# Attention scores as 64-row products, two heads in the two halves of the array, and a rotary step with whole heads in a tile

## The chip, the cores and the metric

The kernel runs on one core of a Trainium2 chip. The metric is the device time of one execution in microseconds (us). Before the change it is 1016.0 us, the median of three runs (1015.67 to 1016.91).

A core has five engines with a queue each, worked off in order: TensorE (PE; its weight loads are shown as PEld), VectorE (DVE), ScalarE (ACT), GpSimd (POOL) and SyncE (SP), which here issues the transfers. Engines wait for each other by semaphores. Matrix products go into eight PSUM banks of 128 x 512 float32; everything else lies in SBUF, 128 partitions wide.

## The reference, cut to what matters

A decoder block on 512 tokens of width 1024, in float32: a SwiGLU part, a token-mixing part, a second SwiGLU part, each behind a modulated RMSNorm. The change is in the token mixing:

```
proj = u @ w_in                      # p (256), q, k, v (768 each), gates (2048)
y_pool = multiscale_pool(p, ...)
q = apply_rope(q.reshape(B, S, 12, 64), cos, sin)      # also k
for gi, (window, dilation) in enumerate(((128, 1), (512, 4), (2048, 16))):
    hs = slice(gi * 4, gi * 4 + 4)                     # four heads of 64 per group
    o, lse = dilated_window_attention(q[:, :, hs], k[:, :, hs], v[:, :, hs], window // dilation, dilation)
y_attn = sum of the groups' outputs, weighted by softmax of their lse
merged = g_pool * (y_pool @ w_pool_branch) + g_attn * (y_attn @ w_attn_branch)
return merged @ w_out

def apply_rope(t, cos, sin):
    t1, t2 = jnp.split(t, 2, axis=-1)
    return jnp.concatenate([t1 * cos - t2 * sin, t2 * cos + t1 * sin], axis=-1)
```

Scores are products over the 64 elements of a head, in float32.

## The kernel before, in words

Dense layers are computed with channels on partitions and tokens on the free axis. To keep float32 accuracy at the speed of the rounded type, each operand is split in a high and a low part, and each product is three: high by high, high by low, low by high (`mm3`, L339 to L343; written out in other loops, L1226 to L1228 and L1276 to L1278). Weights come in 512 KB chunks by SP into three buffers (`fetch`, L226). ACT writes their high part (`split_hi`, L298) and DVE their low part (`split_lo`, L310) into a ring. `look` (L319), called at the start of a tile, fetches and keeps the split three chunks ahead of PE. A tile (`mm_tile`) is 24 products of 128 x 512, one PSUM bank.

`mix` runs the token mixing. All instructions stand in each engine's queue in the order in which this Python code emits them: there is no scheduler behind it. Its stages:

- `head` computes q and k of group 0 in four banks; `rope` (L978) turns them on DVE. A tile holds 32 elements of each of four heads: one tile the first halves, one the second. So a rotation needs two tiles, `pa` and `pb`: four products (L985) and, for each pair of heads, a difference (L991) and a sum (L992), that put both halves of the two heads into 128 rows. `classes` = 4 reorders tokens by residue, for groups 1 and 2.
- v of group 0 (L1226 to L1229).
- Eight tiles with q and k of groups 1 and 2. Between their products PE works on the attention of group 0, as hooks at the step k of the tile (`hooks`, L1236). A unit is a block of 128 queries and a pair of heads (n, hp); there are eight in group 0. A unit's work stands in three tiles: scores at hook 5, transposes of the probabilities at hook 3 of the next tile, products with v at hook 4 of the one after. One unit enters per tile.
- Two tiles for the pooling branch (`pool_diff` on POOL), four wide steps for v of groups 1 and 2 (L1276 to L1282). Beside them the units of groups 1 and 2 (kind 1) run in pairs, hp = 0 and 1.
- Gates, the merge of the groups, and the output.

The scores: the rows of a pair of heads are interleaved by halves, so a product over one head alone needs a copy of q with the other head's rows at zero. `at_prep` (L1014) makes it on DVE (L1022) with a mask of ones and zeros, and `at_scores` (L1026) multiplies over all 128 rows, one product per head (and group): L1039, L1041, L1045. Its result lies in one of two banks (`bS`), by turns. DVE adds the mask and takes maxima (L1057, L1059), ACT takes exponentials (L1062). `at_turn` transposes on PE (L1074) and copies on ACT (L1077, L1080). `at_values` (L1083) multiplies with v on PE (L1097) into a half of the bank `bO`, by hp; in group 0 DVE copies that half out at once (L1099), and in groups 1 and 2 both halves after the second (L1101).

Of the kernel before, what the change touches and what calls it, by code (L numbers as in the profile page):

```python
# [75 lines left out]
    return ins, [np.concatenate(outs[i:i + 2], axis=1) for i in range(0, n, 2)] + outs[n:]  # L76


def qk_cols(base, g, second):
    return np.concatenate([base + (4 * g + h) * 64 + 32 * second + np.arange(32) for h in range(4)])  # L80


def lay_mix(w_in, w_pb, w_ab, w_out):
    ch = []

    def qk(g):
        for base in (256, 1024):
            for s in (0, 1):
                ch.append(_fmajor(w_in, qk_cols(base, g, s)))

    qk(0)
    v = w_in[:, 1792:2560].reshape(KT, P, 768)
    for i in range(2):
        ch.append(v[4 * i:4 * i + 4, :, :256].transpose(1, 0, 2).reshape(P, -1))
    qk(1)
    qk(2)
    for t in range(2):
        ch.append(_fmajor(w_in, np.arange(t * P, (t + 1) * P)))
    for i in range(4):
        ch.append(v[2 * i:2 * i + 2, :, 256:].transpose(1, 0, 2).reshape(P, -1))  # L100
    for m in range(KT + 1):
        if m < KT:
            ch.append(_fmajor(w_in, 2560 + np.arange(m * P, (m + 1) * P)))
            ch.append(_fmajor(w_in, 3584 + np.arange(m * P, (m + 1) * P)))
        if m:
            c = np.arange((m - 1) * P, m * P)
            ch.append(np.concatenate([_fmajor(w_pb, c), _fmajor(w_ab, c)], axis=1))
    for m in range(KT):
        ch.append(_fmajor(w_out, np.arange(m * P, (m + 1) * P)))
    return ch  # L110
# [26 lines left out]
class Kernel:  # L137
# [837 lines left out]
        for b in range(4):  # L975
            self.nc.sync.dma_start(self.cs[32 * b:32 * b + 32], self.scr2)

    def rope(self, pa, pb, dst, classes=1):  # L978

        v = self.nc.vector
        t = [self.rt.tile([P, 528], F32, name=f"rt{i}")[:, :T] for i in range(4)]
        for o, x, y in ((t[0], pa, self.cos), (t[1], pb, self.sin), (t[2], pb, self.cos), (t[3], pa, self.sin)):
            v.tensor_tensor(o, x, y, op=OP.mult)  # L985
        for half in (0, 1):
            rows = slice(64 * half, 64 * half + 64)
            cols = slice(T * half, T * half + T)
            src = [x[rows].rearrange("p (i c) -> p c i", c=classes) for x in t]
            to = [dst[r, cols].rearrange("p (c i) -> p c i", c=classes) for r in (slice(0, 64), slice(64, 128))]  # L990
            v.tensor_tensor(to[0], src[0], src[1], op=OP.subtract)  # L991
            v.tensor_tensor(to[1], src[2], src[3], op=OP.add)  # L992

    def mm_tile(self, hooks=()):

# [15 lines left out]
        kind, n, hp = u  # L1011
        return (1, 2) if kind else (0,), slice(n * P, n * P + P)

    def at_prep(self, u):  # L1014

        kind, n, hp = u
        gs, toks = self.at_tokens(u)
        qz = self.aw.tile([P, T], F32, name="qz")
        for i, g in enumerate(gs):
            q = self.qt[g][:, hp * T:hp * T + T]  # L1020
            for h in range(2):
                self.nc.vector.tensor_scalar(qz[:, (2 * i + h) * P:(2 * i + h + 1) * P], q[:, toks],  # L1022
                                             self.hmask[:, h:h + 1], None, op0=OP.mult)
        self.qz[u] = qz

    def at_scores(self, u):  # L1026
        kind, n, hp = u
        nc = self.nc
        M = nc.tensor.matmul
        self.si ^= 1  # L1030
        S = self.bS[self.si]
        qz = self.qz.pop(u)
        gs, toks = self.at_tokens(u)
        for h in range(2):
            o = h * 256
            if kind == 0:
                k = self.kt[0][:, hp * T:hp * T + T]
                if n == 0:
                    M(S[:, o + P:o + 2 * P], qz[:, h * P:h * P + P], k[:, 0:P], start=True, stop=True)  # L1039
                else:  # L1040
                    M(S[:, o:o + 2 * P], qz[:, h * P:h * P + P], k[:, (n - 1) * P:(n + 1) * P], start=True, stop=True)  # L1041
            else:
                for i, g in enumerate(gs):
                    k = self.kt[g][:, hp * T:hp * T + T]
                    M(S[:, o + i * P:o + i * P + P], qz[:, (2 * i + h) * P:(2 * i + h + 1) * P], k[:, toks],  # L1045
                      start=True, stop=True)
        p = self.aw.tile([P, T], F32, name="prob")
        nb = self.aw.tile([P, 2], F32, name="negmax")
        mask = self.mask[kind]
        c0 = P if (kind == 0 and n == 0) else 0  # L1050
        if kind == 0:
            mx, ls = self.m1[:, 4 * n + 2 * hp:4 * n + 2 * hp + 2], self.l1[:, 4 * n + 2 * hp:4 * n + 2 * hp + 2]
        else:
            mx, ls = self.o23[:, n, 256 + 2 * hp:258 + 2 * hp], self.o23[:, n, 260 + 2 * hp:262 + 2 * hp]
        for h in range(2):
            cs = slice(h * 256 + c0, h * 256 + 256)
            nc.vector.tensor_tensor_reduce(p[:, cs], S[:, cs], mask[:, c0:], 1.0, 3.0 * NEG, op0=OP.add, op1=OP.max,  # L1057
                                           accum_out=mx[:, h:h + 1])
        nc.vector.tensor_scalar(nb, mx, -0.125, None, op0=OP.mult)  # L1059
        for h in range(2):  # L1060
            cs = slice(h * 256 + c0, h * 256 + 256)
            nc.scalar.activation(p[:, cs], p[:, cs], AF.Exp, bias=nb[:, h:h + 1], scale=0.125,  # L1062
                                 accum_out=ls[:, h:h + 1])
        self.prob[u] = p
# [112 lines left out]
    def mix(self):  # L1177
        nc, tc = self.nc, self.tc
        v, M = nc.vector, nc.tensor.matmul
        self.prob, self.probT, self.pd, self.qz = {}, {}, {}, {}  # L1180
        self.si = self.ti = 0
        outer = ExitStack()
        mp = outer.enter_context(tc.tile_pool(name="mx", bufs=1))
        two = lambda pool, n, dt=F32R: [pool.tile([P, T], dt, name=f"{n}{i}") for i in range(2)]
# [1 line left out]
        with tc.tile_pool(name="ma", bufs=1) as ma, tc.tile_pool(name="rt", bufs=1) as self.rt, \  # L1186
# [15 lines left out]

            bk = [self.nb() for _ in range(4)]
            self.head(1, bk, AF.Exp)
            self.rope(bk[0], bk[1], self.qt[0])
            self.rope(bk[2], bk[3], self.kt[0])


            free = [b for b in self.B if b not in bk]
# [6 lines left out]
            for n in range(4):  # L1216
                if n:
                    self.split(self.pos + n - 1)
                    self.fetch()
                if n == 3:  # L1220
                    self.at_prep((0, 0, 0))
                b = self.nb()
                ts = slice(n * P, n * P + P)
                for k in range(KT):
                    hi, lo = w[k]
                    M(b[:, :256], self.UH[k][:, ts], hi, start=k == 0, stop=False)  # L1226
                    M(b[:, :256], self.UH[k][:, ts], lo, start=False, stop=False)
                    M(b[:, :256], self.UL[k][:, ts], hi, start=False, stop=k == KT - 1)  # L1228
                nc.scalar.activation(self.v1[:, n, :], b[:, :256], AF.Copy)  # L1229
# [3 lines left out]

            pipe = [[], []]

            def hooks(new, extra=(), nxt=()):  # L1236
                h = {}
                sc, old = pipe
                for i, u in enumerate(old):
                    h.setdefault(4, []).append(lambda u=u: self.at_values(u))  # L1240
                for i, u in enumerate(sc):
                    h.setdefault(3 + i, []).append(lambda u=u: self.at_turn(u))
                for i, u in enumerate(new):
                    if u not in self.qz:
                        h.setdefault(i, []).insert(0, lambda u=u: self.at_prep(u))
                    h.setdefault(5 + i, []).append(lambda u=u: self.at_scores(u))
                for u in nxt:
                    h.setdefault(6 + len(new) - 1, []).append(lambda u=u: self.at_prep(u))
                for k, f in extra:
                    h.setdefault(k, []).append(f)  # L1250
                pipe[0], pipe[1] = list(new), sc
                return h


            todo = [[(0, n, hp)] for n in range(4) for hp in range(2)]
            for g in (1, 2):
                for dst in (self.qt[g], self.kt[g]):
                    ps = [self.mm_tile(hooks(todo.pop(0), nxt=todo[0] if todo else ())) for s in range(2)]
                    self.rope(ps[0], ps[1], dst, 4)


            g23 = [[(1, c, hp) for hp in range(2)] for c in range(4)]
            b = self.mm_tile(hooks([], nxt=g23[0]))
            self.pool_diff(0, b)
            b = self.mm_tile(hooks(g23[0], nxt=g23[1]))
            self.pool_diff(1, b)
            self.held = self.pos
            w = [x for _ in range(4) for x in self.take()]
# [83 lines left out]
    def build(self):  # L1352
# [21 lines left out]
        self.hpi, self.r4 = tl("hpi", 1), tl("r4", 4)  # L1374
        self.cond = tl("cond", D)
        self.ones = tl("ones", P)
        self.invf, self.hmask, self.icnt, self.ident = cst[:, 0:1], cst[:, 1:3], cst[:, 3:35], cst[:, 35:163]
        self.cst = cst
        self.cs = tl("cs", 2 * T)
        self.cos, self.sin = self.cs[:, :T], self.cs[:, T:]  # L1380
# [142 lines left out]
def constants():  # L1523
    i = np.arange(P)
    invf = (ROPE_THETA ** (-np.arange(0, HEAD_DIM, 2) / HEAD_DIM)).astype(np.float32)
    hm = np.stack([(i % 64 // 32 == h) for h in range(2)], axis=1).astype(np.float32)
    cnt = np.zeros((P, 32), np.float32)
    for t in range(2):
        for half in range(2):
# [2 lines left out]
                np.float32(1) / np.minimum(np.arange(16) + 1, w).astype(np.float32)  # L1532
    neg = lambda ok: np.where(ok, np.float32(0), np.float32(NEG))
    q, k = i[:, None], i[None, :]
    return np.concatenate([invf[i % 32][:, None], hm, cnt, np.eye(P, dtype=np.float32),
                           neg(k >= q), neg(k <= q), neg((k <= q) & ((q - k) % 4 == 0))], axis=1)


# [40 lines left out]
```

## Time and profile before

| | before |
|---|---|
| median of three runs | 1016.0 us |
| the profiled execution, its own time | 1016.32 us |
| its span, first to last instruction | 1014.5 us |
| PE busy | 1003.8 us |
| DVE busy | 764.8 us |
| ACT busy | 442.0 us |
| mean granted PE clock | 0.998 |
| attention of group 0 beside q and k of groups 1 and 2 | 393 to 457 us of the span |
| attention of groups 1 and 2 | 457 to 509 us |

Busy times are sums over the span; PE's are modelled ends of pipelined products, so two may overlap. A view of instructions in order of time gives the start, the duration, engine, line, operation, output and inputs, and in brackets the idle time before it with what ended it. Lines are those of the kernel before, unless "after" is written.

### The profile page before, as it was taken

How to read it: one execution, taken by the hardware profiler on the slowest of the kernel's cores; microseconds unless marked ns; L12 is line 12 of the kernel's file. 1: busy time of each engine (PE TensorE's matmuls, PEld its weight loads, DVE VectorE, ACT ScalarE, POOL GpSimd, SP SyncE). 2: the span in 40 equal slices, each digit the busy share in tenths (PEclk: the TensorE clock that was granted, in tenths of full speed). 3: DMA queues.
4: the chain of work that ended last, by engine and by line, in shares of the span. 5: the costliest groups of instructions: out<-in, count | busy, mean ns of one | idle time of the engine just before them, and what ended most of it. 6: DMA issues, size and time to landing. Idle time of an engine off the chain costs nothing.

```text
span 1014.5 us, 15763 instructions
## 1 busy us (share of the span) xinstructions
PE 1003.8 (99%) x6448; PEld 912.2 (90%) x6448; DVE 764.8 (75%) x1120; ACT 442.0 (44%) x674; POOL 26.1 (3%) x30
## 2 busy tenths in 40 slices
PE   8999999999999999999999999999999999999997
PEld 7888999989899999889988888998899899998997
DVE  7989979789796667878448776577787776676754
ACT  5443644525435443334323333454366254352553
POOL 0000000000000000008000000000000000000001
PEclk9999999999999999999999999999999999999999
DMA  9856456455454323222155773421353234241312
GB/s 336 274 197 214 146 163 221 148 175 168 148 182 136 104 77 104 63 63 84 32 198 188 253 265 107 122 63 62 95 176 122 66 105 146 84 146 43 113 33 83
DMA packets 43114, 139.61 MB, mean 138 GB/s; under 512 B 4897, under 2 KB 8225, under 8 KB 43042
## 3 DMA queue, kind: packets, MB, share of 16 engines
q1 hardware_dynamic: 42354, 137.95, 41.8%
q8 instruction: 50, 0.82, 0.3%
q10 hardware_dynamic: 688, 0.66, 0.2%
q14 instruction: 22, 0.18, 0.1%
HBM read 135.82 MB, written 2.77 MB: 137 GB/s over the span
## 4 chain that ended last, share of the span: by engine, by line
PE 93%; DVE 5%; ACT 1%; issue 1%; DMA 0%; DVEq 0%; ACTq 0%
PE bank L341 16%; PE bank L342 16%; PE bank L343 16%; PE bank L723 10%; PE bank L725 10%; PE bank L724 10%; PE bank L1506 1%; PE bank L1510 1%; PE bank L1508 1%; PE bank L1097 1%; PE bank L1276 1%; DVE wlo L310 1%; PE bank L1277 1%; PE bank L1278 1%; PE bank L1045 1%; PE bank L1074 1%
## 5 line engine op out<-in xcount | busy, mean ns | idle before, releaser
L310 DVE TENSOR_TENSOR wlo<-raw,whi 128x1024 fp32r<-128x1024 f32 (+6 forms) x166 | 174.4, 1062 | 66.5 <-ACT whi L298 65.9
L298 ACT ACTIVATE whi<-raw 128x1024 fp32r<-128x1024 f32 (+6 forms) x166 | 150.0, 920 | 47.6 <-DVE raw L242 41.6
L725 PE MATMUL bank<-UH,wlo 128*128 128x256 f32 x544 | 150.5, 277 | 0.0
L723 PE MATMUL bank<-UH,whi 128*128 128x256 f32 x544 | 150.5, 277 | 0.0
L724 PE MATMUL bank<-UL,whi 128*128 128x256 f32 x544 | 150.5, 277 | 0.0
L341 PE MATMUL bank<-HI,whi 128*128 128x512 f32 (+1 forms) x406 | 146.6, 361 | 0.0
L342 PE MATMUL bank<-HK,whi 128*128 128x512 f32 (+1 forms) x406 | 146.4, 361 | 0.0
L343 PE MATMUL bank<-HI,wlo 128*128 128x512 f32 (+1 forms) x406 | 146.2, 360 | 0.0
L341 PE MATMUL bank<-UH,whi 128*128 128x512 f32 (+1 forms) x400 | 145.9, 365 | 0.0
L343 PE MATMUL bank<-UH,wlo 128*128 128x512 f32 (+1 forms) x400 | 141.8, 355 | 0.5 <-DVE wlo L310 0.5
L342 PE MATMUL bank<-UL,whi 128*128 128x512 f32 (+1 forms) x400 | 141.8, 355 | 0.1
L310 DVE TENSOR_TENSOR wlo<-X,whi 128x1024 fp32r<-128x1024 f32 (+4 forms) x106 | 111.7, 1064 | 33.3 <-ACT whi L298 32.9
L298 ACT ACTIVATE whi<-X 128x1024 fp32r<-128x1024 f32 (+4 forms) x106 | 95.7, 927 | 46.3 <-DVE X L242 45.6
L723 PE MATMUL bank<-SH,whi 128*128 128x256 f32 x408 | 113.8, 279 | 0.1
L724 PE MATMUL bank<-SL,whi 128*128 128x256 f32 x408 | 113.6, 278 | 0.0
L725 PE MATMUL bank<-SH,wlo 128*128 128x256 f32 x408 | 113.6, 278 | 0.0
L724 PEld LDWEIGHTS bank<-UL,whi 128*128 128x128 f32 x544 | 102.3, 188 | 0.3
L723 PEld LDWEIGHTS bank<-UH,whi 128*128 128x128 f32 x544 | 102.1, 188 | 0.3
L725 PEld LDWEIGHTS bank<-UH,wlo 128*128 128x128 f32 x544 | 102.1, 188 | 0.0
L342 PEld LDWEIGHTS bank<-HK,whi 128*128 128x128 f32 x406 | 76.3, 188 | 11.8 <-DVE HK L651 0.4
L341 PEld LDWEIGHTS bank<-HI,whi 128*128 128x128 f32 x406 | 76.5, 188 | 11.5
L343 PEld LDWEIGHTS bank<-HI,wlo 128*128 128x128 f32 x406 | 76.4, 188 | 11.6
(228 smaller groups left out, 1760.2 us busy)
## 6 DMA issues: line engine op xcount, KB each, us to landing
ada<-wada SPq DMA_DIRECT2D x47, 512.0 KB, 5.0
raw<-wmix SPq DMA_DIRECT2D x44, 512.0 KB, 3.6
raw<-wf1i SPq DMA_DIRECT2D x32, 512.0 KB, 4.4
raw<-wf2i SPq DMA_DIRECT2D x30, 512.0 KB, 3.6
X<-wf2i SPq DMA_DIRECT2D x14, 512.0 KB, 3.6
cs<-wada SPq DMA_DIRECT2D x12, 512.0 KB, 3.5
AR<-wada SPq DMA_DIRECT2D x12, 512.0 KB, 4.2
raw<-wf2o SPq DMA_DIRECT2D x12, 512.0 KB, 3.6
```

The source lines that it names most:

```text
L298: self.nc.scalar.activation(self.hi[:, y], r[:, x], AF.Copy)
L310: self.nc.vector.tensor_tensor(self.lo[:, y], r[:, x], self.hi[:, y], op=OP.subtract)
L341: M(ps, hi, uh, start=start, stop=False)
L342: M(ps, hi, ul, start=False, stop=False)
L343: M(ps, lo, uh, start=False, stop=stop)
L723: M(o, hi, uh, start=start and p == 0 and k == 0, stop=False, skip_group_check=True)
L724: M(o, hi, ul, start=False, stop=False, skip_group_check=True)
L725: M(o, lo, uh, start=False, stop=k == 3, skip_group_check=True)
L1045: M(S[:, o + i * P:o + i * P + P], qz[:, (2 * i + h) * P:(2 * i + h + 1) * P], k[:, toks], start=True, stop=True)
L1074: nc.tensor.transpose(b[:, i * P:i * P + P], p[:, i * P:i * P + P], self.ident)
L1097: M(o, pt[:, blk * P:blk * P + P], v, start=i == 0, stop=i == len(srcs) - 1)
L1276: M(b, self.UH[k][:, c::4], hi, start=k == 0, stop=False)
```

## The change

Rows of the projection are laid out by whole heads: a tile now holds two heads of 64, each with its first 32 rows, then its second 32. The rotation works on one tile at a time. ACT copies the bank to SBUF with the sign of the sine term; four transfers on SP's queue exchange the 32-row halves within SBUF; DVE multiplies the bank with the cosines (`rope_a`), and later the exchanged copy with the sines, and adds (`rope_b`). In group 0 all four `rope_a` stand before the four `rope_b`; in groups 1 and 2 each `rope_b` stands right behind its `rope_a`.

The masked copies of q (`at_prep`) are gone. A score product runs over the 64 rows of its head, rows 0 to 63 for the first head and 64 to 127 for the second, each head into a bank of its own, and the two units hp = 0 and 1 of a pair into the halves of these banks. The units of group 0 enter in pairs, one pair every second tile: `todo` holds [pair, nothing, pair, nothing, ...]. Both units' scores stand at hook 5, one behind the other, then both units' maxima and exponentials (`at_exp`). Values are as before in their text: for each unit of the pair at hook 4, products into its half of `bO`, then DVE's copy.

```diff
     def qk(g):
         for base in (256, 1024):
-            for s in (0, 1):
-                ch.append(_fmajor(w_in, qk_cols(base, g, s)))
+            for hp in (0, 1):
+                ch.append(_fmajor(w_in, base + (4 * g + 2 * hp) * 64 + np.arange(P)))
...
-    def rope(self, pa, pb, dst, classes=1):
-        v = self.nc.vector
-        t = [self.rt.tile([P, 528], F32, name=f"rt{i}")[:, :T] for i in range(4)]
-        for o, x, y in ((t[0], pa, self.cos), (t[1], pb, self.sin), (t[2], pb, self.cos), (t[3], pa, self.sin)):
-            v.tensor_tensor(o, x, y, op=OP.mult)
-        for half in (0, 1):
...
+    def rope_a(self, bank, dst, hp, classes, t, w):
+        nc = self.nc
+        nc.scalar.activation(t, bank, AF.Copy, scale=self.sign)
+        for i in range(4):
+            o = i ^ 1
+            nc.sync.dma_start(w[32 * o:32 * o + 32], t[32 * i:32 * i + 32])
+        by = lambda x: x.rearrange("p (i c) -> p c i", c=classes)
+        nc.vector.tensor_tensor(dst[:, hp * T:hp * T + T].rearrange("p (c i) -> p c i", c=classes), by(bank), by(self.cos),
+                                op=OP.mult)
+
+    def rope_b(self, dst, hp, classes, w):
         v = self.nc.vector
+        d = dst[:, hp * T:hp * T + T].rearrange("p (c i) -> p c i", c=classes)
+        v.tensor_tensor(w, w, self.sin, op=OP.mult)
+        v.tensor_tensor(d, d, w.rearrange("p (i c) -> p c i", c=classes), op=OP.add)
...
-    def at_prep(self, u):
...
     def at_scores(self, u):
         kind, n, hp = u
         nc = self.nc
         gs, toks = self.at_tokens(u)
+        for i, g in enumerate(gs):
+            for h in range(2):
+                rows = slice(64 * h, 64 * h + 64)
+                q, k = (x[g][rows, hp * T:hp * T + T] for x in (self.qt, self.kt))
+                if kind:
+                    o, ks = slice(i * P, i * P + P), toks
                 else:
+                    o, ks = (slice(0, 2 * P), slice((n - 1) * P, (n + 1) * P)) if n else (slice(P, 2 * P), toks)
+                S = self.bS[h][:, 2 * P * hp:2 * P * hp + 2 * P]
+                nc.tensor.matmul(S[:, o], q[:, toks], k[:, ks], start=True, stop=True, skip_group_check=True)
...
+            to = [(self.qt[0], 0), (self.qt[0], 1), (self.kt[0], 0), (self.kt[0], 1)]
+            sw = [self.qt[2][:, :T], self.qt[2][:, T:], self.kt[2][:, :T], self.kt[2][:, T:]]
+            for i in range(4):
+                self.rope_a(bk[i], *to[i], 1, self.v23[:, i, :], sw[i])
+            for i in range(4):
+                self.rope_b(*to[i], 1, sw[i])
...
-                for i, u in enumerate(new):
-                    if u not in self.qz:
-                        h.setdefault(i, []).insert(0, lambda u=u: self.at_prep(u))
-                    h.setdefault(5 + i, []).append(lambda u=u: self.at_scores(u))
-                for u in nxt:
-                    h.setdefault(6 + len(new) - 1, []).append(lambda u=u: self.at_prep(u))
+                h.setdefault(5, []).extend(lambda f=f, u=u: f(u) for f in (self.at_scores, self.at_exp) for u in new)
...
-            todo = [[(0, n, hp)] for n in range(4) for hp in range(2)]
+            todo = [x for n in range(4) for x in ([(0, n, hp) for hp in range(2)], [])]
             for g in (1, 2):
                 for dst in (self.qt[g], self.kt[g]):
-                    ps = [self.mm_tile(hooks(todo.pop(0), nxt=todo[0] if todo else ())) for s in range(2)]
-                    self.rope(ps[0], ps[1], dst, 4)
+                    for hp in range(2):
+                        b = self.mm_tile(hooks(todo.pop(0)))
+                        rt = [self.rt.tile([P, 528], F32, name=f"rt{2 * i + hp}")[:, :T] for i in range(2)]
+                        self.rope_a(b, dst, hp, 4, *rt)
+                        self.rope_b(dst, hp, 4, rt[1])
```

`at_exp` is the second part of the old `at_scores`, from the maxima on. The constants hold the signs where the masks of ones and zeros were.

## The prediction, made before the changed kernel had run

> **What bounds the kernel now.** I read the page first, then the waits of TensorE, then the attention part (381 to 515 us) in order of time, engine by engine, then the order of instructions and semaphore waits in both built programs.
>
> ```profile
> span 1014.5 us, 15763 instructions
> PE 1003.8 (99%) x6448; PEld 912.2 (90%) x6448; DVE 764.8 (75%) x1120; ACT 442.0 (44%) x674; POOL 26.1 (3%) x30
> PE 93%; DVE 5%; ACT 1%; issue 1%; DMA 0%; DVEq 0%; ACTq 0%
> ```
>
> TensorE is the bound everywhere: 1003.8 of 1014.5 us busy, 93% of the chain that ended last. So a microsecond taken from its queue is a microsecond gained, and a wait put into its queue is lost in full; the other engines matter only where PE waits for them. In the attention part PE waits only once in a visible way, for an exponential:
>
> ```profile
> 413.98 0.39 PE L343 MATMUL bank<-UH,wlo 128*128 128x512 f32 x1
> 414.61 0.93 PE L1074 MATMUL bank<-cst,prob 128*128 128x128 f32 x4 [0.24 <-ACT prob L1062]
> ```
>
> The start before the gap is 413.98; a 512-column product is followed 0.227 us later, so L1074 could start at 414.21 and started at 414.61; its four pieces then took 0.68 to the next line instead of 0.36. That is 0.7 us, the slack of this schedule at its tightest.
>
> **What the scores cost PE now.** PE in order of time (start, duration):
>
> ```profile
> 409.02 0.40 PE L343 MATMUL bank<-UH,wlo 128*128 128x512 f32 x1
> 409.26 1.02 PE L1041 MATMUL bank<-k,qz 128*128 128x256 f32 x4
> 409.93 0.58 PE L341 MATMUL bank<-UH,whi 128*128 128x512 f32 x1
> 410.36 0.39 PE L342 MATMUL bank<-UL,whi 128*128 128x512 f32 x1
> ...
> 470.82 1.05 PE L1045 MATMUL bank<-k,qz 128*128 128x128 f32 x8
> 471.63 0.60 PE L1276 MATMUL bank<-whi,UH 128*128 128x512 f32 x1
> ```
>
> A float32 product runs as two passes. The 256-column passes stand 0.168 us apart (409.26 to 409.93, four), the 128-column ones 0.10 (470.82 to 471.63, eight); the first wide product after a block is 0.2 us late (409.93 to 410.36 instead of 0.227). A unit costs 0.45 us (n = 0), 0.88 (n > 0) or 1.0 (groups 1 and 2); 2 x 0.45 + 6 x 0.88 + 8 x 1.0 = 14.2 us in all. That is all the change can win from the scores.
>
> **The change, part by part.**
>
> *Scores.* The number of passes stays. The two units of a pair now follow each other in one hook, so half of the late starts go: 3 x 0.2 + 4 x 0.2 + 0.08 = 1.5 us. What two heads in the two halves of the array do is not in the trace. Ceiling: passes in pairs at half the time, 24 x 0.168/2 + 64 x 0.10/2 + 8 x 0.09/2 = 5.6 us. Floor: no gain, and something lost at each of the 16 changes between whole and halved array; the nearest row is the late start of 0.2 us, and with the 0.16 by which a product outlasts its spacing that bounds it at 0.35 each, 5.6 us. I take weight loads as the limit: the closest spacing of any pass here is 0.09 us (transposes L1074, four in 0.36), so 256-column passes fall from 0.168 to 0.09 (24 x 0.078 = 1.9) and 128-column ones by 0.01 (0.6): 2.5 us, less 16 x 0.08 = 1.3 for the changes. Row, then rule: the Trainium skill (TensorEngine Tiling (Array Packing), Key Properties) says that switching the tiling mode drains the TensorE; no trace here shows it. By that rule the late start would be paid on entering as well, 8 x 0.2 = 1.6 in place of 1.3. With the 0.7 us of the exponential's wait (it falls away, below), the scores gain 1.5 + 2.5 - 1.3 + 0.7 = 3.4 us.
>
> *Masked copies (L1022).* 48 DVE operations go, 0.2 to 0.45 us each. PE never waited for them; worth nothing by themselves.
>
> *Rotary step.* Per pair of projection tiles DVE made four products and four half-height operations. Now each tile has one ACT copy (0.60, as L1151), four transfers on SP, and on DVE a product with cosines (strided, 1.08 as L991 in groups 1 and 2), one with sines (0.68 as L985) and an add (1.08). DVE busy falls from 7.0 us per pair (404.31 to 411.5) to 5.7. But DVE now stands still between the first and the second product until the transfers land, and everything behind them in its queue waits: the weight split L310, the copies of the attention output (L1099), the maxima (L1057).
>
> *Group 0.* Four copies end near 382.8, sixteen transfers leave SP from 381.4 at 0.46 us each (to 388.3), land by 390.4; the last two operations end at 391.9, where DVE's L310 began at 391.13 before. PE needs that split near 393.5, and it is there at 393.0: nothing, or 2 us once if transfers land 2 us later.
>
> *Values: the wait that decides.* Units of a pair now turn and multiply in the same tile. Both write halves of one bank (bO), and DVE copies the first half out before the second is written. In the order of the built program PE's first product of the second unit (L1083 after) waits for DVE's copy of the first unit (L1085 after) issued in the same hook. Before, that copy lay a whole tile back (412.69, while PE's next values stood at 416.08). In DVE's queue this copy stands behind the previous tile's rotary step and a weight split:
>
> ```profile
> 410.44 1.07 DVE L992 TENSOR_TENSOR q<-rt,rt 64x512 f32<-64x512 f32 x1
> 411.55 1.23 DVE L310 TENSOR_TENSOR wlo<-raw,whi 128x1024 fp32r<-128x1024 f32 x1
> 412.69 0.28 DVE L1099 COPY o<-bank 128x128 f32<-128x128 f32 x1
> ```
>
> Count from the end of the tile before, 0 = the start of the next tile's first product. ACT starts at 0.2 (a DVE read of a finished bank began 0.20 after, 405.16 to 405.36), ends at 0.8. SP issues four transfers at 0.46 us each (spacing of the four cs<-scr), the fourth at 2.3. Landing:
>
> ```profile
> cs<-scr SPq DMA_DIRECT2D x4, 128.0 KB, 4.2
> out_dram<-out SPq DMA_DIRECT2D x3, 128.0 KB, 1.8
> masks<-cst SPq DMA_DIRECT2D x1, 192.0 KB, 2.4
> ```
>
> No transfer within SBUF is there; bounds 1.8 and 4.2. I take 2.1, between the two rows that did not share the engines: 64 KB rides alone here, since weight loads are issued behind the four. So 4.4, plus 0.1; sine 5.2, add 6.3, split 7.5 (411.55 to 412.69 is 1.14), copy 7.8, PE going again at 8.0 (0.2 as above). PE arrives at 4 x 0.681 + 0.81 = 3.5 (eight passes of values, 423.31 to 424.12; n = 0 has four, 3.1). **Gap: 4.5 us three times, 4.9 once: 18.4 us.** With 1.8 it is 17.2, with 4.2 it is 26.8. While PE stands, DVE catches up, so the exponentials are no longer late.
>
> *The clock in these gaps.* The granted clock after PE's last matmul, which ends at 1007.7 (core: stretch, length, busy times, PEclk, DMA):
>
> ```profile
> 1009.00:1009.50 0.50, 0.00 (x0) 0.00 (x0) 0.50 (x3) 0.00 (x0) 0.50 (x2) 1.00 0.76 260
> 1009.50:1010.00 0.50, 0.00 (x0) 0.00 (x0) 0.50 (x3) 0.00 (x0) 0.50 (x1) 0.90 0.01 2
> 1010.00:1010.50 0.50, 0.00 (x0) 0.00 (x0) 0.38 (x2) 0.00 (x0) 0.09 (x1) 0.50 0.39 135
> ```
>
> It fell to half 2.2 us after the last work. At the start, matmuls ran at the slow duration (421 ns for 128x128, 275 later) from 4.60 to 8.18. A gap of 4.5 us should fall likewise, and 3.6 us at half speed then cost 1.8 us: 4 x 1.8 = 7.2. Bounds: 0, and 2.8 each. The Trainium skill (TensorE: Matmul & The Clock Gate, Part 1) puts the idle window at about 3.4 us, free-running; by that rule a gap of 4.5 holds a whole idle window in only a third of its positions ((4.5 - 3.4) / 3.4, an estimate), and the time would be the first rival's, or between. The tail above agrees with the fall, with less than 3.4 us of idleness.
>
> **Sum**, on the profiled execution (1016.32 us, span 1014.5): 1016.3 + 18.4 - 3.4 + 7.2 = 1038.5. The median of the runs shown is 0.3 lower: **1038 us**.
>
> **Rivals.**
> - *The clock holds in the gaps.* For: the gap is a few us and surrounded by dense work, where the tail was thin. Against: 2.2 us sufficed in the tail. 1016.3 + 18.4 - 3.4 - 0.3 = 1031.
> - *The transfers are slow* (4.2, as cs<-scr): 4 x 2.1 = 8.4 more, 1047. Against: 64 KB is small, nothing else is queued; for: the only row with 32 partitions is that slow one.
> - *The copy comes in time*, and the scores' gain stands alone: 1016.0 - 3.4 = 1013, 1009 with halves fully side by side. It decides if the copy is done within 3.5 us of the tile's end. Even with transfers that land at once the DVE chain alone (0.8 + 1.1 + 0.7 + 1.1 + 1.1 + 0.3) needs 5.1. So this needs the order to act otherwise than built.
> - *Halves are not run side by side at all* (the change does not do what it says): the scores lose up to 4 us instead of gaining; 1038 becomes about 1044.
> - *Floor meets ceiling*: gaps of 2 us and the full 5.6 us: no change.
>
> **How the numbers follow.** Forecast 0.48 (1033 to 1042 by itself), clock holds 0.27, slow transfers 0.12, halves not side by side 0.06, in time 0.04, no change 0.03. Range: from the clock held, landing at 1.8 and half the scores' spread (1027) to slow transfers (1048). About 0.2% (2 us) is what a measurement can tell from no change: faster 0.04, within 0.03, slower 0.93.
>
> **What would show it.** Right: four PE gaps of 4 to 5 us in the tiles with values of the first group, released by DVE's output copy; DVE idle on transfers landing about 2 us after issue; granted clock below 1 right after these gaps; score blocks of eight passes near 0.75 us plus a late start. Wrong: no gaps there (the copy in time); gaps with the clock at 1.00; a PE wait for exponentials or for the weight split instead; score passes no closer than 0.168.

## The result, and the profile after

The changed kernel takes **1043.25 us** (median of five runs, 1042.96 to 1045.41); before, 1016.0. The ratio is 1.0271, with a 95% interval of 1.0261 to 1.0282. The profiled execution has a span of 1041.5 us, 27.0 more than before. From here on lines are those of the changed kernel.

The page: span, busy times, the clock by slices, and shares of the chain that ended last.

```profile
span 1041.5 us, 15814 instructions
...
PE 1010.5 (97%) x6448; PEld 912.5 (88%) x6448; DVE 744.7 (72%) x1060; ACT 449.2 (43%) x686; POOL 25.8 (2%) x30
...
PEclk9999999999999999788999999999999999999998
...
PE 89%; DVE 6%; ACT 2%; SPq 1%; DMA 1%; issue 1%; DVEq 0%; ACTq 0%
```

The number of products on PE is the same, 6448, yet PE is busy for 6.7 us more: in the attention part three slices have less than nine tenths of the clock. DVE is less busy than before (744.7 against 764.8) and has a larger share of the chain (6% against 5%), with SP's queue and DMA new beside it. So less work, but more of it in PE's way. What PE waited for (output and line, releaser: total us, times, longest):

```profile
PE bank L1083 <- DVE o L1085: 18.4, 4, 4.9
PE bank L339 <- DVE wlo L306: 2.5, 2, 2.0
```

The first row is new: the four gaps. The second was a single wait of 0.5 us in the kernel before:

```profile
PE bank L343 <- DVE wlo L310: 0.5, 1, 0.5
```

The other of the two, of 2.0, is new. The wait for an exponential is gone. The second gap, PE and DVE in order of time:

```profile
434.11 0.69 DVE L989 TENSOR_TENSOR rt<-rt,cs 128x512 f32<-128x512 f32 x1 [2.65 <-DMA rt<-rt]
...
435.82 1.22 DVE L306 TENSOR_TENSOR wlo<-raw,whi 128x1024 fp32r<-128x1024 f32 x1
436.95 0.28 DVE L1085 COPY o<-bank 128x128 f32<-128x128 f32 x1
437.39 0.88 PE L1083 MATMUL bank<-v,probT 128*128 128x64 f32 x3 [4.50 <-DVE o L1085]
```

Read it upwards: PE stood for 4.50 us until DVE had copied 128 columns in 0.28; the copy stood behind a weight split, and this behind a product that had waited 2.65 us for a transfer. DVE was not short of time; its queue was held.

The clock, in stretches of 3.41 us (core: stretch, length, busy PE, PEld, DVE, ACT, POOL, then PEclk, DMA share, GB/s):

```profile
432.05:435.46 3.41, 0.83 (x8) 0.69 (x7) 1.32 (x2) 0.00 (x0) 0.00 (x0) 1.00 0.61 181
435.46:438.87 3.41, 1.48 (x7) 1.51 (x8) 1.78 (x3) 0.00 (x0) 0.00 (x0) 0.50 0.08 28
438.87:442.29 3.42, 3.42 (x14) 2.21 (x13) 0.29 (x1) 0.00 (x0) 0.00 (x0) 0.50 0.00 0
```

PE was idle from 432.89 to 437.39; half clock held from 435.46 to 442.29, 6.83 us, of which 4.9 were work. The three other gaps have half clock at 414.98 to 421.81, 459.35 to 466.18 and 479.83 to 486.66, 6.83 us each. In all, PE worked 23.0 us at half clock; there the wide products start 0.427 us apart instead of 0.227, so these 23.0 us hold work of 12.2 and 10.8 are lost.

The transfers (line, queue, operation: issue in ns, least, median, most; then KB each and median us to landing):

```profile
L981 SPq DMA_DIRECT2D rt<-rt x32: 507/584/1363, 403.9 to 476.6; - x32
```

```profile
rt<-rt SPq DMA_DIRECT2D x32, 64.0 KB, 2.0
```

And the stall behind group 0, at the first tile (only two lines of the stretch are shown):

```profile
393.70 2.69 DVE L306 TENSOR_TENSOR wlo<-raw,whi 128x1024 fp32r<-128x1024 f32 x3
...
394.98 0.50 PE L339 MATMUL bank<-UH,wlo 128*128 128x512 f32 x1 [2.00 <-DVE wlo L306]
```

DVE's splits of that stage begin only at 393.70, behind the last rotary add (393.09), because sixteen transfers at 0.59 us each left SP until 390.9. Between two wide starts of PE the stall is 2.2 us (2.40 less a step of 0.23).

### The profile page after: what moved, and what is told of

Same layout as the page of the kernel before. It is cut to its first block, busy times and chain, and to the rows that moved or that the text cites. A ratio compares the mean times of both kernels' runs of the same rounds, so it can differ in the third digit from the quotient of the medians.

```text
span 1041.5 us, 15814 instructions
## 1 busy us (share of the span) xinstructions
PE 1010.5 (97%) x6448; PEld 912.5 (88%) x6448; DVE 744.7 (72%) x1060; ACT 449.2 (43%) x686; POOL 25.8 (2%) x30
## 4 chain that ended last, share of the span: by engine, by line
PE 89%; DVE 6%; ACT 2%; SPq 1%; DMA 1%; issue 1%; DVEq 0%; ACTq 0%
PE bank L337 16%; PE bank L339 16%; PE bank L338 16%; PE bank L719 10%; PE bank L721 10%; PE bank L720 10%; PE bank L1493 1%; PE bank L1495 1%; PE bank L1497 1%; SPq L981 1%; PE bank L1083 1%; DVE wlo L306 1%; PE bank L1027 1%; PE bank L1263 1%; DMA rt<-rt 1%
## 5 line engine op out<-in xcount | busy, mean ns | idle before, releaser
L719 PEld LDWEIGHTS bank<-UH,whi 128*128 128x128 f32 x544 | 102.1, 188 | 0.3
L721 PEld LDWEIGHTS bank<-UH,wlo 128*128 128x128 f32 x544 | 102.1, 188 | 0.0
L339 PEld LDWEIGHTS bank<-UH,wlo 128*128 128x128 f32 x400 | 76.2, 191 | 14.5 <-DVE wlo L306 3.4
L337 PEld LDWEIGHTS bank<-UH,whi 128*128 128x128 f32 x400 | 76.5, 191 | 12.6 <-issue 2.3
```

Source lines behind the costliest of these rows:

```text
L337: M(ps, hi, uh, start=start, stop=False)
L339: M(ps, lo, uh, start=False, stop=stop)
L719: M(o, hi, uh, start=start and p == 0 and k == 0, stop=False, skip_group_check=True)
L721: M(o, lo, uh, start=False, stop=k == 3, skip_group_check=True)
```

## The experiments

Unless said otherwise, each kernel is the changed one with the edit shown. "Blocks" are taken from PE's starts in order of time: from the wide product ahead of a block to the second one behind it, less the two wide steps (0.45). Ratios are to runs of the kernel before that were made beside each experiment (medians of 1016.1 to 1016.6 us).

### One copy behind the second unit

```diff
-        if kind == 0:
-            self.nc.vector.tensor_copy(self.o1[:, n, P * hp:P * hp + P], O)
-        elif hp == 1:
-            self.nc.vector.tensor_copy(self.o23[:, n, :256], self.bO[:, :256])
+        if hp == 1:
+            self.nc.vector.tensor_copy((self.o23 if kind else self.o1)[:, n, :256], self.bO[:, :256])
```

> The changed kernel, but in group 0 DVE copies both halves of bO out at once behind the second unit, as in groups 1 and 2; no product of a pair then waits for a copy of its own hook. Theory (the wait for the copy, and the clock that it costs, make the loss): the four gaps of 18.4 us go, the granted clock stays at 1.00 in 413 to 490 us, and with it go some 11 us of half speed (about 23 us after restart at 0.50); what stays is the stall of 2.2 us at the first tile behind v of group 0 and the scores' gain of about 5. 1043.2 - 18.4 - 11 = 1014, 1011 to 1017. Rival (the next late thing takes the wait's place): DVE is still some 5 us late at the maxima, PE then waits for exponentials (L1060 after), and the time stays over 1022.

Measured: 1016.21 us (ratio to before 1.0002, 0.9993 to 1.0011), within the theory's range at its upper end. The four gaps and their half clock are gone, and with them 27.0 us: this one wait, with the clock behind it, made the loss. But the rival holds in part. Transposes in this kernel, then in all_rows (below), where they don't wait:

```profile
418.76 0.93 PE L1060 MATMUL bank<-cst,prob 128*128 128x128 f32 x4
```

```profile
417.07 0.62 PE L1060 MATMUL bank<-cst,prob 128*128 128x128 f32 x4
```

The block takes 0.3 us more than it needs, and two such tiles lose 0.44 and 0.50 between their wide steps: PE waits for the exponentials there. That DVE is late with the maxima because the transfers hold it is shown only by both_orders (below), where this goes. The stall behind group 0 stays, and here it drew the clock down as well, which in the profiled execution of the changed kernel it did not:

```profile
392.70:396.11 3.41, 1.43 (x7) 0.91 (x7) 3.30 (x4) 0.39 (x1) 0.00 (x0) 1.00 0.00 0
396.11:399.52 3.41, 3.41 (x10) 2.63 (x9) 1.56 (x3) 0.50 (x1) 0.00 (x0) 0.50 0.88 287
```

### The gaps filled with idle products

```diff
+            if kind == 0 and hp == 1 and h == 0:
+                for _ in range(19):
+                    M(self.bS[0], self.UH[0][:, :P], self.UH[1], start=True, stop=True, skip_group_check=True)
             for i, (blk, v) in enumerate(srcs):
```

> The changed kernel, with 19 idle products of 128 x 512 (into a bank of scores that is free then; their result is not used) between the values of the first and the second unit of a group-0 pair. 19 x 0.227 = 4.3 us, as long as the gap of 4.5, so PE is busy while it would wait. Theory (half speed after the gaps costs about 11 us over the gaps themselves): the granted clock stays at 1.00 through the four places and the time falls to about 1032, 1029 to 1035, though more is computed. Rival (the 27 us of span are the gaps and other waits, and the clock adds nothing, or 7.2 as predicted): 1043, or 1036.

Measured: 1035.93 us (1033.24 to 1039.11; ratio 1.0192, 1.0172 to 1.0212). The ratios of this kernel and of the changed one differ by 0.0079, 8 us; the profiled execution (1033.24, the fastest of four that scatter by 5.9) is 10.0 us ahead of the changed kernel's where the attention ends (523.91 against 533.91 at the same product). PE's place of the first gap:

```profile
410.31 4.59 PE L1084 MATMUL bank<-UH 128*128 128x512 f32 x19
415.41 0.63 PE L1086 MATMUL bank<-v,probT 128*128 128x64 f32 x4 [0.52 <-DVE o L1088]
```

The clock stayed at 1.00 through all four places. 76 more products made the kernel faster: the half clock behind the gaps costs 8 to 10 us beyond the gaps. The median (1035.9) lies just above the theory's range and at the rival's 1036, so by itself it does not exclude 7.2. Against 7.2 speak the traces: the 10.0 here, and the 10.8 lost in the changed kernel's work at half clock.

### The second half of the rotary step a tile later

```diff
-                        b = self.mm_tile(hooks(todo.pop(0)))
+                        b = self.mm_tile(hooks(todo.pop(0), late))
...
-                        self.rope_b(dst, hp, 4, rt[1])
+                        late = [(6, lambda a=(dst, hp, 4, rt[1]): self.rope_b(*a))]
```

> The changed kernel with the wait kept as it is, but rope_b of each tile of groups 1 and 2 (the product with sines, which waits for the transfers, and the add) stands at hook 6 of the next tile, behind the copies, the scores and the maxima in DVE's queue. Theory (the copy was late because of what stands before it in DVE's queue): only the first unit's own copy is waited for; PE's first four or eight passes, 0.20 until DVE starts, 0.28 for the copy, 0.20 back: gaps of about 0.7 us four times, too short for the clock, 1043.2 - 18.4 - 11 + 2.8 = 1017, 1013 to 1021. Rival (the copy waits for something that moves with it, the bank or a transfer): gaps stay at 4 us or more, 1035 to 1045.

Measured: 1018.79 us (ratio 1.002, 1.0011 to 1.0029).

```profile
PE bank L1083 <- DVE o L1085: 2.4, 4, 1.0
```

18.4 us became 2.4, with the wait itself untouched: the copy was late by what stood ahead of it in DVE's queue. The clock stayed at 1.00 in these four places, and the time fell by 24.5 us, 8.5 more than the gaps (16.0).

### Without the transfers

```diff
-        for i in range(4):
-            o = i ^ 1
-            nc.sync.dma_start(w[32 * o:32 * o + 32], t[32 * i:32 * i + 32])
...
-                        self.rope_b(dst, hp, 4, rt[1])
+                        self.rope_b(dst, hp, 4, rt[0])
```

> The changed kernel without the 48 transfers: DVE multiplies ACT's signed copy itself with the sines, so the exchange of the halves is left out and the rotation is another one. Order and waits of everything else stay. Theory (two thirds of the gap are the transfers, the rest is DVE's own queue): DVE's chain takes 5.1 us from the tile's end, PE arrives at 3.5, so gaps of about 1.8 three times and 2.2 once, 7.6 us, too short for the clock in most places; the stall of 2.15 at the first tile goes. 1043.2 - 10.8 - 10 - 2.2 = 1020, 1017 to 1025. Rival (the transfers are all of it, DVE overlaps its chain with PE's first products): no gap, 1011 to 1014.

Measured: 1024.01 us (ratio 1.0081, 1.0067 to 1.0095). The gaps are 6.4 us in all, the longest 1.9, against 7.6 expected: some two thirds of the gaps were the transfers, one third DVE's own queue. The stall behind group 0 is gone. But three of four places drew the clock down, where I had expected few, and the time is in the upper part of the range.

### Nine idle products: what makes the clock fall

```diff
-                for _ in range(19):
+                for _ in range(9):
```

> fill_gap with 9 idle products instead of 19: 2.0 us filled, about 2.6 us of idleness left in each of the four places. Theory (the clock is set at the ends of windows of 3.4 us on a fixed grid, as the falls and rises in the changed kernel lie at 415.0, 421.75, 435.5, 442.2, 459.3, 466.2, 479.8 and 486.6, and a window with idleness in more than about half is enough): two or three of the four places fall, the others not, by how the window lies; stretches of half clock of 3.4 or 6.8 us; 1036 to 1041. Rival (a whole idle window is needed): no place falls, 1033 to 1036. Rival (any gap over 2.2 us): all four, 1041 to 1044.

Measured: 1042.26 us (ratio 1.0258, 1.0242 to 1.0273), 1 us above the theory's range and in that of the last rival; its trace speaks for the theory: PE waited 10.1 us in four places, the longest 2.8, and three places fell. The first, which did not, then the third, which did (windows on the grid that this execution's falls and rises give):

```profile
413.14:416.55 3.41, 1.79 (x8) 1.12 (x6) 2.10 (x3) 0.00 (x0) 0.00 (x0) 1.00 0.63 175
416.55:419.96 3.41, 2.27 (x15) 1.62 (x15) 1.28 (x3) 0.00 (x0) 0.00 (x0) 1.00 0.00 0
...
457.51:460.92 3.41, 1.04 (x9) 1.07 (x10) 2.22 (x4) 0.00 (x0) 0.00 (x0) 1.00 0.13 53
```

The first gap lies across the end of a window (idle for 0.48 and 0.33 of the two), the third mostly in one (0.70). Part of why the time came out higher than I worked out: the stall behind group 0 fell too in this execution (half clock from 396.07 to 399.48), which the expectation did not count.

Over all profiled executions in which the clock fell, the windows ahead of a fall were idle for 0.43 to 1.00, and other windows at full clock for up to 0.48. The two lowest that fell and the one at 0.43 that did not are all in no_transfers (0.43, 0.45 and 0.43 in the order shown):

```profile
425.02:428.44 3.42, 1.94 (x14) 1.67 (x12) 3.16 (x5) 0.00 (x0) 0.00 (x0) 1.00 0.04 17
...
442.09:445.50 3.41, 1.86 (x15) 1.67 (x14) 2.79 (x5) 0.00 (x0) 0.00 (x0) 1.00 0.00 0
...
462.57:465.98 3.41, 1.93 (x16) 1.82 (x16) 2.15 (x4) 0.00 (x0) 0.00 (x0) 1.00 0.23 22
```

The second of these was followed by 6.83 us at half clock, the third by 3.41, the first by none. So about half a window is the mark, and idleness as the trace models it is not the whole of it.

### What the halves are worth

```diff
-                rows = slice(64 * h, 64 * h + 64)
+                rows = slice(0, P)
```

> The kernel copy_after_pair, with each score product over all 128 rows of its pair of heads, unmasked: both heads get the sum over the pair, so the attention leaves out the separation of the two heads; number, columns and places of the passes stay. Theory (halves side by side gain 0.04 per 128-column pass and 0.07 per 256-column pass, and about 0.1 is lost at each change of mode): 64 x 0.042 + 24 x 0.07 + 8 x 0.04 = 4.7, less 16 x 0.1 = 1.6: 3 us slower than copy_after_pair, 1.5 to 4.5; 128-column passes stand 0.10 apart and the first product behind a block is less late than 0.34. Rival (the gain came from the pairing of the units alone, halves and mode changes cancel out): within 1 us of it.

Measured: 1017.78 us (ratio 1.0011, 1.0002 to 1.002), 1.6 us behind copy_after_pair where 3 was expected. The blocks in the trace say 3.4: a pair costs 0.90 (n = 0), 1.74 (n > 0), 1.80 and 1.92 (groups 1 and 2: the first pair, and the other three) with all rows, and 0.86, 1.28, 1.30 and 1.43 in halves. Of the rest, 0.94 went into the waits for exponentials in copy_after_pair, whose PE came earlier to a DVE that was no earlier; the remainder lies within the runs' scatter and the clock behind group 0, and is not told apart here. To see the whole of it the other waits had to go.

### Both orders mended

copy_after_pair, with the four `rope_b` of group 0 moved behind the loop over v:

```diff
-            for i in range(4):
-                self.rope_b(*to[i], 1, sw[i])
...
                 nc.scalar.activation(self.v1[:, n, :], b[:, :256], AF.Copy)
+            for i in range(4):
+                self.rope_b(*to[i], 1, sw[i])
             self.held = None
```

> The kernel copy_after_pair, and in group 0 the four rope_b stand behind the loop over v of group 0 instead of ahead of it, so the weight splits of that loop no longer stand behind products that wait for the sixteen transfers. Theory (the stall of 2.15 us at the first tile, and the half clock that follows it in some executions, come from that place in DVE's queue): stall gone, clock 1.00 in 393 to 400; 1016.2 - 2.15 - 0.7 (half of the 1.5 to 1.9 that the clock took in the execution profiled there) = 1013.4, 1012 to 1015. Rival (the first tile's split is late because its weights or its high part are late behind sixteen issues on SP): PE waits there as long as before, 1016.

Measured: 1015.84 us (ratio 0.9993, 0.9984 to 1.0002), a miss. The stall for the split is gone and the clock holds, but PE's first scores now wait for the rotary step (L1027 for L990, 0.8 us; the block takes 2.2 instead of 0.86), two transposes wait for exponentials (0.80 and 1.12 between wide steps instead of 0.36), and a new 0.5 is lost on a weight split. The lateness moved. With `rope_b` of groups 1 and 2 a tile later as well:

> group0_order, and rope_b of each tile of groups 1 and 2 at hook 6 of the next tile, as in rope_b_later; the copy of both halves behind the second unit stays. Theory (what was left were waits that transfers pass on through DVE's queue): the two stretched transposes (0.80 and 0.86 in place of 0.36, waiting for exponentials) go too, no wait of PE is left in this part, and against before there remain 3.8 us of scores and the 0.7 of its exponential: 1016.4 - 3.8 - 0.7 = 1012, 1011 to 1013.5. Rival (one more stage behind moves the lateness to the scores of groups 1 and 2 or to weight splits): a new wait of PE, 1014 to 1017.

Measured: **1013.04 us** (1012.8 to 1013.65; ratio 0.9969, 0.9956 to 0.9981). The stretched transposes are gone; of the waits the 0.8 at the first scores is left. This is 0.3% less than the kernel before, and the interval leaves out 1. The same with all 128 rows:

> both_orders, with each score product over all 128 rows, unmasked, so that the attention leaves out the separation of the two heads, as in all_rows. Theory (halves are worth 0.04 + 3 x 0.46 + 4 x 0.49 = 3.4 us on PE, as the blocks of all_rows and copy_after_pair stood in the traces, and nothing is left that eats it): 3.4 us slower than both_orders, 2.5 to 4.5. Rival (PE's gain is given back elsewhere, as the 1.6 between copy_after_pair and all_rows suggests): 0 to 2 us slower.

Measured: 1016.58 us (ratio 1.0, 0.9991 to 1.0009): 3.5 us slower, as the blocks say. With the other waits the same in both kernels, the halves are worth in time what the blocks say.

### Are they side by side?

Scores of groups 1 and 2 (start, duration; the next line gives the block's end), in both_orders:

```profile
488.96 1.16 PE L1027 MATMUL bank<-k,q 64*128 64x128 f32 x16
490.05 0.62 PE L1262 MATMUL bank<-whi,UH 128*128 128x512 f32 x1
```

in both_orders_all_rows:

```profile
492.16 1.95 PE L1027 MATMUL bank<-k,q 128*128 128x128 f32 x16
493.86 0.60 PE L1262 MATMUL bank<-whi,UH 128*128 128x512 f32 x1
```

Sixteen passes take 1.09 and 1.70 us, 0.068 and 0.106 each. Two experiments settle whether that is two passes at a time, both on both_orders. All products in one half:

```diff
-                rows = slice(64 * h, 64 * h + 64)
+                rows = slice(0, 64)
```

> both_orders, with every score product over rows 0 to 63, so that the second head's scores are those of the first and its own are left out: passes of 64 rows as before, but all in one half of the array. Theory (a pass is no faster by itself; two run side by side in the two halves): blocks are as long as with all 128 rows, 16 passes of 128 columns in about 1.70 instead of 1.09 and 8 of 256 columns in 1.54 instead of 1.06, and the time 2.5 to 4 us over both_orders. Rival (64 rows alone make a pass cheaper, as the small loss of both_orders_heads_apart lets one think): 1.1 and 1.06, no difference.

Measured: 1019.01 us (ratio 1.0029, 1.0018 to 1.004), 6.0 us slower than both_orders.

```profile
493.95 2.05 PE L1027 MATMUL bank<-k,q 64*128 64x128 f32 x16
495.93 0.62 PE L1262 MATMUL bank<-whi,UH 128*128 128x512 f32 x1
```

Sixteen passes of 64 rows in one half take 1.98 us, more than those of 128 rows (1.70). So the whole gain is that two run side by side; a half by itself is a loss. The starts of the passes show both. What has started up to 0.05 us into a block, in both_orders, then in one_half:

```profile
488.96 0.38 PE L1027 MATMUL bank<-k,q 64*128 64x128 f32 x2
```

```profile
493.95 0.37 PE L1027 MATMUL bank<-k,q 64*128 64x128 f32 x1
```

In both_orders two passes start within 0.01 us, and the next two behind them. In one_half the passes start one by one, 0.111 apart (256 columns: 0.216), exactly as over 128 rows. A block in one half is nevertheless 0.39 us longer than over 128 rows (2.13 against 1.74, 2.31 against 1.92): the second pass starts 0.1 later, and the wide products on both sides stand further off. I take that as the price of changing between whole and halved array and back; with it the scores add up (below). It was not in the 2.5 to 4 us expected; the blocks of the two traces differ by 6.3, the times by 6.0. And the heads not alternating:

```diff
-        for i, g in enumerate(gs):
-            for h in range(2):
+        for h in range(2):
+            for i, g in enumerate(gs):
```

> both_orders, but in groups 1 and 2 a unit's four score products run head 0 of both groups, then head 1 of both, instead of alternating. Theory (only a pass that follows one of the other half overlaps it; the second pass of the same product does not): of the 15 steps between the 16 passes of a pair, 7 change the half when heads alternate and 3 here; a step that changes costs 0.03, one that does not 0.107, so the 16 passes take 1.09 + 4 x 0.075 = 1.39 us and the time is 4 x 0.3 = 1.2 us more. Rival (a product over 64 rows is cheaper by itself, whatever it follows): 16 passes in 1.09, no difference.

Measured: 1013.52 us (ratio 0.9971, 0.9961 to 0.9981), 0.5 slower than both_orders by the medians and 0.2 by the spans, with intervals that overlap. The trace is clearer: sixteen passes take 1.19 us instead of 1.09, where the theory asked for 1.39 and the rival for 1.09. one_half excludes the rival's reason. So passes run side by side also when four passes of one half stand between two changes. The block's first two passes start 0.01 us apart here too, so PE seems to look at least four passes ahead; the trace does not name the half of a pass, and how much further it looks no run here shows.

### The best version

both_orders, with `rope_b` of group 0 spread over the loop:

```diff
                 nc.scalar.activation(self.v1[:, n, :], b[:, :256], AF.Copy)
+                for i in ((), (0,), (1,), (2, 3))[n]:
+                    self.rope_b(*to[i], 1, sw[i])
             self.held = None
```

> both_orders, with the four rope_b of group 0 not all behind the loop over v of group 0, but the first behind its step 1, the second behind step 2 and two behind step 3: DVE stood idle there 1.65 and 1.01 us, and the transfers of those tiles had landed. Theory (in both_orders PE's first scores, 2.10 us in place of 0.74, wait for the last of these four on DVE): this wait of 1.3 us goes, 1013.0 - 1.3 = 1011.7, 1011 to 1012.6. Rival (a product of rope_b now delays a weight split of that loop): PE waits for wlo instead, 1013 or more.

Measured: **1012.24 us** (1011.11 to 1012.89; ratio 0.9961, 0.9949 to 0.9974). The block of the first scores is back at 0.85, and PE's waits are those of the kernel before without its exponential.

## Why the prediction was right

Its forecast was 1038 with four gaps of 18.4 us, and the kernel took 1043.25 with four gaps of 18.4 us. The time is inside the stated range (1027 to 1048) but 1 us above the band that the forecast had for itself (1033 to 1042), and nearer to the 1044 of the rival without halves side by side; it is the traces that decide for the forecast's mechanism. By its own steps, on the span's 27.0 us:

| step | predicted | measured | from |
|---|---|---|---|
| four waits for DVE's copy | +18.4 | +18.4 | waits of PE |
| half clock behind them | +7.2 | +8 to 10.8 | fill_gap, by medians 8 and by traces 10; 23.0 us of work at half clock |
| scores, pairs together | -1.5 | -0.4 | blocks of all_rows against before |
| scores, halves less changes | -1.2 | -3.4 | blocks; both_orders_all_rows 3.5 |
| wait for an exponential | -0.7 | -0.7 | gone from the waits |
| group 0 | "nothing, or 2 us" | +2.2 | first tile |

With 10.8 for the clock the right column gives 18.4 + 10.8 - 3.8 - 0.7 + 2.2 = 26.9 of the 27.0.

**The wait.** Right in place, cause and size, and shown: taking the wait away (copy_after_pair) and taking away what stood ahead of the copy (rope_b_later) remove the gaps (the second all but 2.4 us) and the half clock behind them. The chain ran nearly as worked out: from the next tile's first product at 429.17, the sine product at 4.9 (4.5 predicted), the copy at 7.8 (7.5), PE at 8.2 (8.0), and PE's first unit ended 0.2 later too. Landing was 2.0 us (2.1 taken), and the issue 0.58 (0.46 taken). That the sum is right to the tenth is luck: both ends of the gap came 0.2 late.

**The clock.** Right in kind; the term was mis-sized. I took 3.6 us at half speed per gap, from the start of the span. I had not read that row to its end: matmuls of 421 ns start there until 9.46, and those of 275 from 9.85, so slow work lasted 5.2 us from 4.60, which would have given some 10 us for four gaps. It was 4.6 to 6.8 us of work per gap, because half clock lasts whole windows of 3.41, two of them behind each gap: 6.83 us. The Trainium skill (TensorE: Matmul & The Clock Gate, Part 1) has such windows, free-running and of about 3.4 us, and the times of falls and rises here agree: all lie on one grid in each execution. It also says that the clock falls after one idle window or more; here the measurement differs: a window that was idle for 0.57 was enough (rope_b_later, fill_9). Of the four gaps here two held a window idle for 0.99 or more, the others one of 0.76 and one of 0.67, and the clock fell behind all four, not behind a third of them as that rule's estimate had it. The rival in which the clock holds fell with them.

**The scores.** The sum was near (3.4 predicted with the exponential, 4.5 measured), its parts were not. I read passes of 256 columns as 0.168 us apart, with a late start of 0.2 behind each block that pairing saves. They start 0.216 apart in the trace, the next wide product starts 0.03 behind the last of them, and the late start is that last pass's own length (eight passes in a row take 1.54, not 8 x 0.168, in all_rows); pairing saved 0.4. And I took 0.09 us, the spacing of the transposes, as a limit that weight loads set. No such limit showed: in halves two passes start every 0.111 us (128 columns) or 0.216 (256), twice the rate. Against that stands the change between whole and halved array, 0.39 us a block (one_half) where I had 0.08 for each of 16. So both terms were too small: 72 x 0.111 / 2 + 24 x 0.216 / 2 = 6.6 us gained instead of 2.5, and 8 x 0.39 = 3.1 lost instead of 1.3; that is 3.5, and 3.4 was measured. That the sum of all parts came near is luck. The sign "blocks of eight passes near 0.75 us" did not come: eight of 256 columns took 1.06. The rival in which the halves are not run side by side is excluded by one_half.

**Group 0.** I let the landing time decide ("2 us once if transfers land 2 us later"). The landing was right; what made it late was the issue, 16 x 0.13 = 2 us more than I had counted. With no slack behind it, this small row decided. That stall is also of a length at which the clock falls in some executions and not in others, by how the window lies: of the six profiled executions that have it, three fell (idle for 0.57 to 0.58 of one window), three did not (in the changed kernel 0.45 and 0.14, across two).

**The rival "the copy comes in time".** Its price was right: 1013 to 1009; with the waits mended the scores' gain stands alone at 1013.0 and 1012.2. The change's idea was sound, and where it put the copy and the rotary step turned it into a loss.

Open: what exactly a window counts (no_transfers has 0.43 with and without a fall), why half clock lasts one window in some places and two in others, and how far ahead PE runs passes of the other half.

## What to carry to other kernels

A wait added on the bottleneck engine costs what stands ahead of the releasing instruction in its engine's queue, not what that instruction takes: a copy of 0.28 us cost 4.5. So put transfers' consumers behind everything that the bottleneck waits for, and share one bank between two units only if it is read out behind the second. When a gap of more than about half a clock window is in sight, count the clock too: here each microsecond of gap cost another half.

## What the runs showed of the hardware

- Half clock came and went on a grid of 3.41 us in every profiled execution in which it came between matmuls, for one or two windows; work that keeps PE busy in a gap, even useless work, can pay (76 products made the kernel 8 us faster).
- float32 passes of 128 columns start 0.111 us apart over 128 rows and over 64 rows in one half alike, and two at a time with both halves at work; of 256 columns, 0.216. Changing from the whole array to halves and back costs 0.39 us a block, so a block gains only if its passes save more than that.
- A transfer within SBUF of 32 rows by 2 KB landed 2.0 us after its issue and took SP 0.58 us to issue; 48 of them are 28 us of SP's queue.
